# A decoder layer on one NeuronCore: the order of two products, a remade weight difference, a chunk-wise end and other banks for the query

## The chip, the cores and the metric

The kernel runs on one core of one Trainium2 chip, as one program without collectives. What is compared is the device time of one execution, in microseconds, as the median of several executions. One further execution was recorded by the profiler; the traces and rows below are of that one. About 0.2% of the time, 2.3 us, is what a measurement of this kernel can tell from no change.

## The reference, cut to what matters

One layer on a residual stream x of 1024 tokens by 1024 features, all in float32.

```
h = rmsnorm(x, pre_mix_g);  z = h @ w_in            # 7 slices of 512 columns
q, f, i, g, gate_b, gate_c, conv_h = split(z)
mix_a = hgrn2(q, f, i, g)                           # 4 heads of 128, gated recurrence
mix_b = gate_b * causal_dwconv(gate_c * conv_h, conv_w)
x = x + rmsnorm(concat(mix_a, mix_b) @ w_out, post_mix_g)
h = rmsnorm(x, pre_ffn_g)
u = causal_dwconv(h @ ffn_w_up, ffn_conv_w)         # 1024 -> 2 * 2816, three taps
gate, val = split(u)
y = (silu(gate) * val) @ ffn_w_down                 # 2816 -> 1024
x = x + rmsnorm(y, post_ffn_g)
```

## The kernel before

Every float32 operand is split into a high part `hi` (type float32r, written by ScalarE) and a low part `lo = x - hi` (written by VectorE; `split`, L112). A product is then three matmuls, hi·hi, hi·lo and lo·hi (`mm3_fm` L166, `mm3_tm` L171). In both, one of the three needs the low part of the weights, and that one comes after a matmul that needs only the high part. A matmul writes a tile of 128 by 512, which fills one PSUM bank.

**Start (L600 to L642).** The input is normalised late: the first projections work on x times its gain, and the factor r of each token comes in when a projection is read out. `gemm_quad` (L184) computes 512 columns in four banks. Its weights come in four pairs of 128 rows; a pair's high and low parts (`h_f`, `l_f` for the forget gate, `h_q`, `l_q` for the query) live in one of three slots, so the third query pair takes the slot that the last forget pair leaves. While the forget projection f runs, the sum of squares is made (`stats_by_feature`, L258, matmuls `pc`), `rstd` (L139) turns it into r by a chain of eleven small VectorE operations on `rt` and `rs`, and `by_token` (L272) lays r out along the tokens: VectorE makes four diagonal tiles `dg`, four 128x128 products `pb` sum them (eight pieces in the trace), and ScalarE copies the result to `rb`. `evac_f` (L296) multiplies the four banks of f by `rb` into `tf` and makes F and the keys by two sigmoids each. Then q follows in the same pool of four banks, `ps_mm`; the other four banks, `ps_ax`, serve small results (`aux`, L104). The second half of the tokens gets its row by `by_token_through_dram` (L283): a write of r to DRAM, element by element, and a read that broadcasts it to all partitions.

**Up projection (L680 to L910).** Both feed-forward matmuls use a scheme with seven products P1 to P7 on 2x2 blocks (the Strassen-Winograd scheme), with sums and differences of blocks as operands. A group n handles a 128-column slice of the gate and one of the values. Its tiles `g` (`pG`) and `v` (`pV`) are "two" tiles of two banks each (`two_banks`, L740). Every product is 12 matmuls. P1 and P2 of the groups 0 to 7 are done ahead, during the output projection, and parked (`ahead`, L704); in the loop `take_back` (L767) copies them into `g`. `mid` (L787) runs P6 into g[:,1], copies that out (`snap`, tile `s`), runs P5 into v[:,1], adds v[:,0] = v[:,1] + s (L799), runs P7 into g[:,1], copies again and adds v[:,1] += s (L802). In the next turn of the loop `tail_1` (L815) adds P4 to g[:,1] and reads out the gate (`conv`, silu), and `tail_2` (L822) adds P3 to v[:,0], reads out the value, multiplies both, and after every second group writes the seven left operands of the down projection to DRAM (`down_operands`, L832; L840 to L842 on SyncE's queue).

**Down projection (L913 to L1069).** The seven products run in the order 1, 2, 6, 7, 5, 3, 4 over eleven 128-row blocks, in six granules `GR` of two rows, one of them of one row (L913). `down_granule` (L973) loads the left operand `s`, and `right_operand` (L947) loads raw blocks b11, b12, b21, b22 of the weights (`raw_w`, five slots) and makes differences: T1 = b12 - b11 in product 1 (for the first two granules, whose product-1 operands were loaded early, in product 2), T2 = b22 - T1 and T3 = b22 - b12 in product 2. T1, T2 and T3 stay in memory; products 5, 6 and 7 use them. Results go into two "two" tiles: chunks 0 and 1 in `pXv` or `pYv`, chunks 2 and 3 in `pXg` or `pYg`. The last product, 4, takes its last three granules as one run (`joined=3`): first all their blocks for chunks 0 and 1, then for chunks 2 and 3. `result` (L1015) reads a chunk (ScalarE squares with a sum, `jy`; VectorE multiplies by the gain, `my`), and `finish_rows` (L1028) does `rstd`, adds the residual (two operations L1037 a chunk) and stores.

**What sets the order.** The framework plans it before the run: on each engine it takes, by its own estimate of times, the instruction that is ready and stands first in the program (`high_priority` goes ahead). On the chip each engine then follows that list strictly, with waits for what it reads or overwrites. Nearly all loads and stores are issued by SyncE (SP), in one list.

Of the kernel before, what the change touches and what calls it, by code (L numbers as in the profile page):

```python
# [17 lines left out]
P = 128  # L18
D = 1024
# [22 lines left out]
def decoder_kernel(ctx: ExitStack, tc: tile.TileContext, x, xT, w_sq, w_cv, w_out, w_up, w_dn,  # L42
# [27 lines left out]
    nc.vector.tensor_scalar(neg[:], vec[:, V_PREF : V_PREF + KH], -1.0, None, ALU.mult)  # L70
# [113 lines left out]
    def gemm_quad(src, act, name, token_major, groups, order=None, pieces=1, rate=1, hooks=None, queue=None,  # L184
                  gains=None):

        order = order or list(range(len(act)))
        pss = [ps_mm.tile([P, TH], F32, tag="mm", name=f"p_{name}_{j}") for j in range(4)]
        ws, i0 = {}, 0
        for gi, n in enumerate(groups):  # L190
            ks = range(i0, i0 + n)
            for i in ks:
                if i // 2 not in ws:
                    ws[i // 2] = load_w(src[order[i] // 2], (P, 2, TH), f"{name}_{i // 2}", pieces,
                                         queue if i == 0 else None, (gains or {}).get(order[i] // 2))
            for j in range(4):
                for i in ks:
                    whi, wlo = (w[:, i % 2, :] for w in ws[i // 2])
                    js = slice(j * P, (j + 1) * P)
                    ahi, alo = act[order[i]]  # L200
                    first, last = i == 0, i == len(act) - 1
                    if token_major:
                        mm3_tm(pss[j][:], ahi[:, js], alo[:, js], whi, wlo, first, last)
                    else:
                        mm3_fm(pss[j][:], whi[:, js], wlo[:, js], ahi, alo, first, last)
                if (i0 + n) % 2 == 0 and j % (4 // rate) == 4 // rate - 1:
                    tick()
            i0 += n
            if hooks and gi in hooks:
                hooks[gi]()  # L210
        return pss
# [6 lines left out]


    lbt = zp.tile([P, 4, H], F32, name="lbt")  # L220
    lbp = vec[:, V_LB : V_LB + H]
    e_, s_, lb, oml = (lbt[:, i, :] for i in range(4))
    nc.vector.tensor_tensor(e_, lbp, lbp, ALU.subtract)
    nc.scalar.activation(e_, e_, AF.Exp)
    nc.vector.reciprocal(s_, e_)
    nc.vector.tensor_tensor(s_, s_, e_, ALU.mult)
    nc.vector.tensor_tensor(lb, s_, s_, ALU.subtract)
    nc.vector.tensor_scalar(oml, lb, -1.0, 1.0, ALU.mult, ALU.add)
# [384 lines left out]

    first = {}
# [8 lines left out]
    def scale_a_rows():  # L623
        with tc.high_priority():
            first["rows"] = by_token(0, first["r"])

    pss = gemm_quad(w_sq[0], Lazy(), "f0", False, (1, 1, 1, 1, 1, 1, 1, 1), pieces=2, queue=nc.scalar,
                    hooks={6: scale_a, 7: scale_a_rows})
    r0 = first["r"]
    rb0 = first["rows"]  # L630
    rq0 = for_values(0, r0)
    F0, UW0 = evac_f(0, pss, rb0)
    pss = gemm_quad(w_sq[1], act_a, "q0", False, PAIRS)
    evac_q(0, pss, rb0, UW0)
# [62 lines left out]
    AHEAD = 8  # L697

# [64 lines left out]
    def head_2(n):  # L763
        b = box[n]
        product(b["g"][:, 0], b.pop("x"), 0, 2)
# [49 lines left out]
    def tail_1(n):  # L815
        b = box[n]
        product(b["g"][:, 1], b["y"], 0, 4)
# [4 lines left out]
    def tail_2(n):  # L822
        b = box[n]
        product(b["v"][:, 0], b.pop("y"), 1, 3)
# [68 lines left out]
    for n in range(NF + 1):  # L893
# [8 lines left out]
        if n:  # L902
            tail_1(n - 1)
        if n >= AHEAD and not last:
            head_2(n)
        if n:
            tail_2(n - 1)
# [27 lines left out]
    def raw_w(kh, nh, i, n, name):  # L935
        t = ft("wr", (P, 2, TH), name, 5)
        nc.sync.dma_start(t[:, :n], w_dn[kh, nh, :, i : i + n])
        return t
# [7 lines left out]

    def right_operand(op, gi, i, n):  # L947

        nm = f"{op}_{gi}"
        if op == 1:  # L950
            b = raw_w(0, 0, i, n, f"b11_{nm}")
            t_1(gi, n, b, raw_w(0, 1, i, n, f"b12_{nm}"))
            return b
        if op == 2:
            b = raw_w(1, 0, i, n, f"b21_{nm}")
            b12 = raw_w(0, 1, i, n, f"b12_{nm}")
            if gi < EARLY:
                t_1(gi, n, raw_w(0, 0, i, n, f"b11_{nm}"), b12)
            b22 = raw_w(1, 1, i, n, f"b22_{nm}")
            t2 = ts[2, gi] = t_slot(2, gi, n)  # L960
            t3 = ts[3, gi] = t_slot(3, gi, n)
            nc.vector.tensor_tensor(t2[:], b22[:, :n], ts[1, gi][:], ALU.subtract)
            nc.vector.tensor_tensor(t3[:], b22[:, :n], b12[:, :n], ALU.subtract)
# [7 lines left out]
        return ts[{5: 1, 6: 2, 7: 3}[op], gi]  # L971

    def down_granule(op, gi):  # L973
        i, n = GR[gi]
        s = ft("sr", (P, 2, TH), f"s{op}_{gi}", 4)
# [10 lines left out]
    def down_product(op, pss, first=False, joined=0, made=()):  # L986
# [3 lines left out]
        for gis in runs:  # L990
            ks = [(gi, k, t) for gi in gis
                  for k, t in enumerate(made[gi] if gi < len(made) else down_granule(op, gi))]
            for cs in ((0, 1), (2, 3)):
# [34 lines left out]
    def finish_rows(hf, cs):  # L1028
        c0, c1 = cs[0], cs[-1] + 1
        r = rstd(ssq[hf][:, c0:c1], D, f"y{hf}{c0}", ssq[hf][:, 4 + c0 : 4 + c1])  # L1030
# [104 lines left out]
```

## Time and profile before

| | |
|---|---|
| median of 3 executions | 1139.5 us (1139.35 to 1140.95) |
| profiled execution: own time, span | 1138.99 us, 1137.2 us |
| TensorE matmul busy (PE) | 1109.6 us, 5096 matmuls |
| VectorE busy (DVE) | 838.4 us |
| ScalarE busy (ACT) | 512.6 us |
| mean granted TensorE clock | 0.994 |
| DMA | 163.03 MB, mean 143 GB/s |

The profiled execution's time is 1.8 us more than its span, which begins with the first recorded instruction. Busy times of the engines overlap. A matmul's end is modelled: its own duration of 0.39 us is more than the 0.227 us between two starts, so a busy PE is judged by the distance between starts and not by the busy time.

### The profile page before, as it was taken

What the parts mean: (1) busy time and instruction counts of PE and PEld (TensorE: products, weight loads), DVE (VectorE), ACT (ScalarE), POOL (GpSimd) and SP (SyncE); (2) the same over time, 40 slices, a digit from 0 to 9 for tenths busy, and PEclk for the clock granted to TensorE, in tenths of its full rate; (3) what the DMA queues carried; (4) which work ended last, traced back from release to release, by engine and by line L of the source; (5) the groups of instructions that cost most, each with busy time, mean ns of one, the idle gap of its engine ahead of it and who ended that gap; (6) DMA issues with size and microseconds to landing.
All of it is one profiled execution on the core that took longest, in us unless ns stands there. A gap on an engine that the chain in (4) does not pass through costs nothing.

```text
span 1137.2 us, 13444 instructions
## 1 busy us (share of the span) xinstructions
PE 1109.6 (98%) x5096; PEld 912.8 (80%) x5096; DVE 838.4 (74%) x1181; ACT 512.6 (45%) x750; POOL 9.7 (1%) x16
## 2 busy tenths in 40 slices
PE   8999999999999999999999999999999999999996
PEld 6878888888878888887777888888888877888884
DVE  8578767636687777387998987878887777744786
ACT  6543335425432337366555444444444433544441
POOL 2000000000000000000000000000000000000000
PEclk9999999999999999999999999999999999999998
DMA  8522223335322238174444323222331479735653
GB/s 292 172 78 74 75 93 113 119 95 201 101 66 86 82 111 260 59 256 167 164 168 168 111 94 139 102 75 102 131 110 51 153 282 334 280 102 168 202 165 132
DMA packets 54432, 163.03 MB, mean 143 GB/s; under 512 B 5856, under 2 KB 6112, under 8 KB 51424
## 3 DMA queue, kind: packets, MB, share of 16 engines
q1 hardware_dynamic: 53936, 161.57, 41.5%
q8 instruction: 40, 0.66, 0.2%
q10 hardware_dynamic: 432, 0.61, 0.2%
q14 instruction: 24, 0.20, 0.1%
HBM read 127.82 MB, written 34.34 MB: 143 GB/s over the span
## 4 chain that ended last, share of the span: by engine, by line
PE 86%; DVE 6%; DMA 3%; ACT 3%; issue 2%; DVEq 0%; SPq 0%; ACTq 0%
PE pG L167 8%; PE pG L169 8%; PE pG L168 8%; PE pV L167 4%; PE pV L169 4%; PE pV L168 4%; PE sl L382 2%; PE p_wo L174 2%; PE p_wo L173 2%; PE p_wo L172 2%; DMA b<-w_dn 2%; PE pXv L173 2%; PE pXv L174 1%; PE pXv L172 1%; PE p_ch L169 1%
## 5 line engine op out<-in xcount | busy, mean ns | idle before, releaser
L113 ACT CAST hs<-s 128x1024 fp32r<-128x1024 f32 (+1 forms) x40 | 39.1, 976 | 91.9 <-PE pXg L173 35.9
L114 DVE TENSOR_TENSOR ls<-s,hs 128x1024 fp32r<-128x1024 f32 (+1 forms) x40 | 45.2, 1129 | 44.4 <-ACT hs L113 44.2
L114 DVE TENSOR_TENSOR l_b<-w,h_b 128x1024 fp32r<-128x1024 f32 x22 | 26.9, 1223 | 33.6 <-ACT h_b L113 33.6
L167 PE MATMUL pG<-uhi,h_x 128*128 128x512 f32 x112 | 44.4, 396 | 0.0
L168 PE MATMUL pG<-ulo,h_x 128*128 128x512 f32 x112 | 44.3, 395 | 0.0
L169 PE MATMUL pG<-uhi,l_x 128*128 128x512 f32 x112 | 44.1, 394 | 0.0
L749 ACT COPY s<-pG 128x512 f32<-128x512 f32 x44 | 25.7, 583 | 40.8 <-PE pG L169 40.6
L114 DVE TENSOR_TENSOR l_t<-t,h_t 128x1536 fp32r<-128x1536 f32 x22 | 38.6, 1755 | 5.9 <-ACT h_t L113 5.7
L811 ACT ACTIVATE g<-pG,vec 128x1024 f32<-128x1024 f32 x22 | 24.5, 1116 | 34.2 <-PE pG L169 34.2
L167 PE MATMUL pG<-c4h,h_b 128*128 128x512 f32 x88 | 35.4, 402 | 4.7 <-ACT s L749 4.7
L820 ACT ACTIVATE g<-g 128x1024 f32<-128x1024 f32 x22 | 23.3, 1061 | 36.3 <-DVE g L813 36.1
L113 ACT CAST h_t<-t 128x1536 fp32r<-128x1536 f32 x22 | 32.6, 1484 | 14.4 <-DVE t L783 9.6
L113 ACT CAST h_x<-w 128x1024 fp32r<-128x1024 f32 x14 | 14.7, 1052 | 47.4 <-DMA w<-w_up 47.4
L383 DVE COPY_PREDICATED S<-m_lev,sl 128x512 f32<-128x512 uint8 x28 | 24.9, 890 | 14.7 <-PE sl L382 14.7
L369 ACT COPY lhs<-UW 128x512 f32<-128x512 f32 x28 | 18.6, 663 | 37.2 <-DVE UW L390 37.2
L382 PEld LDWEIGHTS sl<-UW,lhs 128*128 128x128 f32 x224 | 28.8, 190 | 7.3 <-issue 4.1
L169 PE MATMUL pG<-c4h,l_b 128*128 128x512 f32 x88 | 34.6, 393 | 0.0
L167 PE MATMUL pV<-c3h,h_b 128*128 128x512 f32 x88 | 34.5, 392 | 0.0
L167 PE MATMUL pG<-c7h,h_t 128*128 128x512 f32 x88 | 34.4, 391 | 0.1
L169 PE MATMUL pV<-c3h,l_b 128*128 128x512 f32 x88 | 34.4, 391 | 0.0
L169 PE MATMUL pG<-c7h,l_t 128*128 128x512 f32 x88 | 34.3, 390 | 0.0
L168 PE MATMUL pG<-c4l,h_b 128*128 128x512 f32 x88 | 34.3, 390 | 0.0
(351 smaller groups left out, 3524.1 us busy)
## 6 DMA issues: line engine op xcount, KB each, us to landing
w<-w_up SPq DMA_DIRECT2D x22, 1024.0 KB, 4.8
s<-s_d SPq DMA_DIRECT2D x33, 512.0 KB, 3.9
b<-w_dn SPq DMA_DIRECT2D x33, 512.0 KB, 6.0
s_d<-g SPq DMA_DIRECT2D x22, 512.0 KB, 2.9
s_d<-S SPq DMA_DIRECT2D x11, 768.0 KB, 3.4
r_wo<-w_out SPq DMA_DIRECT2D x16, 512.0 KB, 3.5
xT<-xT SPq DMA_DIRECT2D x16, 256.0 KB, 4.0
r_q<-w_sq SPq DMA_DIRECT2D x8, 512.0 KB, 4.3
```

Source lines behind the costliest of these rows:

```text
L113: nc.scalar.copy(hi, src)
L114: nc.vector.tensor_tensor(lo, src, hi.bitcast(F32), ALU.subtract)
L167: nc.tensor.matmul(ps, whi, ahi, start=first, stop=False, skip_group_check=more)
L168: nc.tensor.matmul(ps, whi, alo, start=False, stop=False, skip_group_check=more)
L169: nc.tensor.matmul(ps, wlo, ahi, start=False, stop=last, skip_group_check=more)
L172: nc.tensor.matmul(ps, ahi, whi, start=first, stop=False, skip_group_check=more)
L173: nc.tensor.matmul(ps, ahi, wlo, start=False, stop=False, skip_group_check=more)
L174: nc.tensor.matmul(ps, alo, whi, start=False, stop=last, skip_group_check=more)
L382: nc.tensor.matmul(pv[:, :, i], lhs[:, i, :], rhs, start=True, stop=True)
L383: nc.vector.copy_predicated(view(S, 2 * X, o + h, (X - h, 2), (2 * h, n), (1, h)), m_lev[:, li].rearrange("p x g (b h) -> p x (g b) h", h= ...
L749: nc.scalar.copy(t[:], ps)
L811: nc.scalar.mul(a[:], c, wc[2])
```

## The change

Five things are edited.

1. In the groups that ran ahead (loop turns 1 to 7) P3 stands in front of P4 in the program; after them P4, gate, P2 of the next group, P3, value keep their order.
2. T3 is no longer kept. Product 7 loads b12 and b22 again and subtracts. T1 of the first two granules is made in product 1, with loads of their own, at granules 2 and 3, so that product 2 loads only b21 and b22. The slots of raw weights go from 5 to 8 and those of left operands from 4 to 6.
3. The joined last granules of product 4 run chunk by chunk, and the last half of the rows is finished one chunk at a time, each with its own `rstd`. The two sums of `rstd` change places.
4. The query projection goes into the banks of `ps_ax`, and the row r of the first half goes through DRAM, read out with `evac_f` after the first pair of the query.
5. The constants of the lower bound (`lbt`) and `neg` are made later in the program.

```
     def gemm_quad(..., gains=None, banks=None):
-        pss = [ps_mm.tile([P, TH], F32, tag="mm", name=f"p_{name}_{j}") for j in range(4)]
+        pss = [banks(f"p_{name}_{j}") if banks else ps_mm.tile([P, TH], F32, tag="mm", name=f"p_{name}_{j}")
+               for j in range(4)]
...
     def scale_a_rows():
-        with tc.high_priority():
-            first["rows"] = by_token(0, first["r"])
+        first["rows"] = by_token_through_dram(0, first["r"])
+        first["FU"] = evac_f(0, pss, first["rows"])
     pss = gemm_quad(w_sq[0], Lazy(), "f0", False, (1, 1, 1, 1, 1, 1, 1, 1), pieces=2, queue=nc.scalar,
-                    hooks={6: scale_a, 7: scale_a_rows})
+                    hooks={6: scale_a})
     r0 = first["r"]
-    rb0 = first["rows"]
+    qss = gemm_quad(w_sq[1], act_a, "q0", False, PAIRS, hooks={0: scale_a_rows}, banks=aux)
+    rb0, (F0, UW0) = first["rows"], first["FU"]
     rq0 = for_values(0, r0)
-    F0, UW0 = evac_f(0, pss, rb0)
-    pss = gemm_quad(w_sq[1], act_a, "q0", False, PAIRS)
-    evac_q(0, pss, rb0, UW0)
+    evac_q(0, qss, rb0, UW0)
...
-        if n:
-            tail_1(n - 1)
-        if n >= AHEAD and not last:
-            head_2(n)
-        if n:
-            tail_2(n - 1)
+        if n and n < AHEAD:
+            product_3(n - 1)
+            product_4(n - 1)
+            gate(n - 1)
+            value(n - 1)
+        elif n:
+            product_4(n - 1)
+            gate(n - 1)
+            if not last:
+                head_2(n)
+            product_3(n - 1)
+            value(n - 1)
...
-        t = ft("wr", (P, 2, TH), name, 5)
+        t = ft("wr", (P, 2, TH), name, 8)
...
+    def early_t1(gi):
+        i, n = GR[gi]
+        t_1(gi, n, raw_w(0, 0, i, n, f"b11_t{gi}"), raw_w(0, 1, i, n, f"b12_t{gi}"))
     def right_operand(op, gi, i, n):
         if op == 1:
+            if gi < 2 * EARLY:
+                early_t1(gi - EARLY)
             b = raw_w(0, 0, i, n, f"b11_{nm}")
             t_1(gi, n, b, raw_w(0, 1, i, n, f"b12_{nm}"))
             return b
         if op == 2:
             b = raw_w(1, 0, i, n, f"b21_{nm}")
-            b12 = raw_w(0, 1, i, n, f"b12_{nm}")
-            if gi < EARLY:
-                t_1(gi, n, raw_w(0, 0, i, n, f"b11_{nm}"), b12)
             b22 = raw_w(1, 1, i, n, f"b22_{nm}")
             t2 = ts[2, gi] = t_slot(2, gi, n)
-            t3 = ts[3, gi] = t_slot(3, gi, n)
             nc.vector.tensor_tensor(t2[:], b22[:, :n], ts[1, gi][:], ALU.subtract)
-            nc.vector.tensor_tensor(t3[:], b22[:, :n], b12[:, :n], ALU.subtract)
+            return b
+        if op == 7:
+            b12 = raw_w(0, 1, i, n, f"b12_{nm}")
+            b = raw_w(1, 1, i, n, f"b22_{nm}")
+            nc.vector.tensor_tensor(b[:, :n], b[:, :n], b12[:, :n], ALU.subtract)
             return b
...
-        s = ft("sr", (P, 2, TH), f"s{op}_{gi}", 4)
+        s = ft("sr", (P, 2, TH), f"s{op}_{gi}", 6)
...
-            for cs in ((0, 1), (2, 3)):
+            for cs in ((0,), (1,), (2,), (3,)) if len(gis) > 1 else ((0, 1), (2, 3)):
...
-        r = rstd(ssq[hf][:, c0:c1], D, f"y{hf}{c0}", ssq[hf][:, 4 + c0 : 4 + c1])
+        r = rstd(ssq[hf][:, 4 + c0 : 4 + c1], D, f"y{hf}{c0}", ssq[hf][:, c0:c1])
...
-    for cs in ((0, 1), (2, 3)):
-        for c in cs:
-            result(1, 0, c, bx[c])
-        finish_rows(1, cs)
+    for c in range(NC_H):
+        result(1, 0, c, bx[c])
+        finish_rows(1, [c])
```

`product_4` and `product_3` are the matmuls that `tail_1` and `tail_2` began with, `gate` and `value` the rest of them.

More of the change, by code (lines that the diff above doesn't have):

```diff
@@ L69, in decoder_kernel @@
     neg = cp.tile([P, KH], F32, name="neg")
-    nc.vector.tensor_scalar(neg[:], vec[:, V_PREF : V_PREF + KH], -1.0, None, ALU.mult)
     nc.scalar.activation(warm[:], ones[:, 0:1], AF.Exp)
@@ L184, in gemm_quad @@
     def gemm_quad(src, act, name, token_major, groups, order=None, pieces=1, rate=1, hooks=None, queue=None,
-                  gains=None):
+                  gains=None, banks=None):
         order = order or list(range(len(act)))
-        pss = [ps_mm.tile([P, TH], F32, tag="mm", name=f"p_{name}_{j}") for j in range(4)]
+        pss = [banks(f"p_{name}_{j}") if banks else ps_mm.tile([P, TH], F32, tag="mm", name=f"p_{name}_{j}")
+               for j in range(4)]
         ws, i0 = {}, 0
@@ L217, in zt @@
         return pool.tile(list(shape), dt, tag=tag, bufs=bufs, name=name or tag)
[L220 to L228, printed above, removed]
     S = zt("S", (P, 2, 8, C))
@@ L612, in __getitem__ @@
             return act_a[k]
+    lbt = zp.tile([P, 4, H], F32, name="lbt")
+    lbp = vec[:, V_LB : V_LB + H]
+    e_, s_, lb, oml = (lbt[:, i, :] for i in range(4))
+    nc.vector.tensor_tensor(e_, lbp, lbp, ALU.subtract)
+    nc.scalar.activation(e_, e_, AF.Exp)
+    nc.vector.reciprocal(s_, e_)
+    nc.vector.tensor_tensor(s_, s_, e_, ALU.mult)
+    nc.vector.tensor_tensor(lb, s_, s_, ALU.subtract)
+    nc.vector.tensor_scalar(oml, lb, -1.0, 1.0, ALU.mult, ALU.add)
     first = {}
@@ L697, in decoder_kernel @@
     AHEAD = 8
+    nc.vector.tensor_scalar(neg[:], vec[:, V_PREF : V_PREF + KH], -1.0, None, ALU.mult)
     ah_w = zh.tile([P, 2, 2, KH, P], F32, tag="F", name="ah_w")
@@ L813, in conv, with product_4, product_3, gate @@
         nc.vector.scalar_tensor_tensor(a[:, 2:], c[:, : T - 2], wc[0], a[:, 2:], ALU.mult, ALU.add)
-    def tail_1(n):
+    def product_4(n):
+        product(box[n]["g"][:, 1], box[n]["y"], 0, 4)
+    def product_3(n):
+        product(box[n]["v"][:, 0], box[n]["y"], 1, 3)
+    def gate(n):
         b = box[n]
-        product(b["g"][:, 1], b["y"], 0, 4)
         g = b["o"] = ft("ag", (P, T), f"g{n}", 3, pool=pa[0])
@@ L820, in tail_1, with value @@
         nc.scalar.activation(g[:], g[:], AF.Silu)
-    def tail_2(n):
+    def value(n):
         b = box[n]
-        product(b["v"][:, 0], b.pop("y"), 1, 3)
         v = ft("av", (P, T), f"v{n}", 2, pool=pa[0])
@@ L970, in right_operand @@
             return b
-        return ts[{5: 1, 6: 2, 7: 3}[op], gi]
+        return ts[{5: 1, 6: 2}[op], gi]
     def down_granule(op, gi):
         i, n = GR[gi]
-        s = ft("sr", (P, 2, TH), f"s{op}_{gi}", 4)
+        s = ft("sr", (P, 2, TH), f"s{op}_{gi}", 6)
         nc.sync.dma_start(s[:, :n], s_d[:, S_AT[op], i : i + n])
```

## The prediction

> **What bounds the kernel now.** I read the page first, then who waited for whom on PE, then timelines of the places that the diff touches.
>
> ```profile
> span 1137.2 us, 13444 instructions
> ...
> PE 1109.6 (98%) x5096; PEld 912.8 (80%) x5096; DVE 838.4 (74%) x1181; ACT 512.6 (45%) x750; POOL 9.7 (1%) x16
> ```
> ```profile
> PE pG L167 <- ACT s L749: 4.7, 7, 0.7
> ...
> PE pb L278 <- DVE dg L277: 1.9, 1, 1.9
> ```
>
> PE bounds it, and the number of large matmuls stays. So the change can only win what PE loses between matmuls and in the tail behind the last one, about 1% of the span. Of PE's waits, the seven on `s` and the one at `pb` are what edits 1 and 4 aim at. I take each stage's loss from distances between starts.
>
> **Start (edits 4 and 5).**
>
> ```profile
> 23.57 0.48 PE L169 MATMUL p_f<-hi,l_f 128*128 128x512 f32 x1
> ...
> 26.61 0.39 PE L167 MATMUL p_f<-hi,h_f 128*128 128x512 f32 x1
> 28.87 1.16 PE L278 MATMUL pb<-dg,ones 128*128 128x128 f32 x8 [1.87 <-DVE dg L277]
> 29.78 0.48 PE L168 MATMUL p_f<-lo,h_f 128*128 128x512 f32 x1
> ...
> 34.45 0.39 PE L167 MATMUL p_q<-hi,h_q 128*128 128x512 f32 x1
> ```
> ```profile
> 4.48 0.17 DVE L70 TENSOR_SCALAR neg<-vec 128x4 f32<-128x4 f32 x1 [1.86 <-DMA vec<-vecs]
> ...
> 5.69 0.75 DVE L244 SCALAR_TENSOR_TENSOR lo<-xT,vec,hi 128x512 fp32r<-128x512 f32 x1
> ...
> 28.04 0.16 DVE L155 SCALAR_TENSOR_TENSOR rs_x<-rt_x,rs_x 128x4 f32<-128x4 f32 x1
> ...
> 32.68 2.66 DVE L303 TENSOR_TENSOR tf<-p_f,rb 128x512 f32<-128x512 f32 x4 [2.15 <-PE p_f L169]
> ...
> 38.67 1.22 DVE L114 TENSOR_TENSOR l_q<-r_q,h_q 128x1024 fp32r<-128x1024 f32 x1
> ```
>
> `pb` stands amid the forget matmuls. From 26.61 to 29.78 are 3.17 us where 0.23 is normal (the pitch is worked out below): 2.9 us go with `pb`. q then starts at 31.5. The constants leave the way of the first low part, 4.48 to 5.69; they can slip back in while it waits for ScalarE, so between 0 and 0.4 us, and I take 0. The other banks cost nothing: the next user of those banks is work that needs q read out anyway.
>
> The change adds a wait. `tf` on VectorE now waits for a row that travels through DRAM; behind it stand the scalings of F and the keys and perhaps `l_q`. On SP, the read waits for the write; behind it are loads for the projections after q, needed when q ends at 53 (31.5 + 4 x 5.46 us, below). The rows for both trips come from the second half of the tokens, then one for a full queue:
>
> ```profile
> rd<-rs_x SPq DMA_DIRECT2D x1, 2.0 KB, 8.7
> ```
> ```profile
> DMA to landing us min/median/max: 3.9/3.9/3.9
> ```
> ```profile
> xs<-x SPq DMA_DIRECT2D x1, 512.0 KB, 7.5
> ```
>
> The row lands at R = 28.2 + 8.7 + 3.9 = 40.8, up to 3.6 later if one of the trips meets a queue like that of `xs` (7.5 - 3.9), so 44.4; I take the middle, 42.4. From `tf` to the end of the next `l_q` were 38.67 + 1.22 - 32.68 = 7.2 us. A query pair takes 24 matmuls, 5.46 us; the third needs its low part at 31.5 + 10.9 + 0.45 = 42.9, the fourth at 48.3. The third's slot is free at 31.5, so it can be split before the row is there; the fourth's only at 37, so it will stand behind. Stall: R - 41.1, 0 to 3.3, and I take 1.3. Start: 2.9 - 1.3 = 1.6 us gained, between -0.4 and 3.3.
>
> The Trainium skill (DMA: Bandwidth & Descriptors, section "Anatomy of one DMA") gives a fixed cost of about 2 us for any DMA; by it the row would land near 33, the stall would be nil and the sum 1.3 better. The 8.7 us for 2 KB differ, and the measurement decides; the same page (Rules for kernel authors) says that a strided last dimension becomes one descriptor per element, as in this write.
>
> **P3 before P4 (edit 1).** One group, with P7's last matmul first:
>
> ```profile
> 561.09 0.39 PE L169 MATMUL pG<-c7h,l_t 128*128 128x512 f32 x1
> 562.15 0.50 PE L167 MATMUL pG<-c4h,h_b 128*128 128x512 f32 x1 [0.68 <-ACT s L749]
> 562.49 0.39 PE L168 MATMUL pG<-c4l,h_b 128*128 128x512 f32 x1
> ...
> 565.00 0.39 PE L167 MATMUL pV<-c3h,h_b 128*128 128x512 f32 x1
> ...
> 567.73 0.39 PE L167 MATMUL pG<-c2h,h_t 128*128 128x512 f32 x1
> ```
> ```profile
> 562.13 0.70 DVE L802 TENSOR_TENSOR pV<-pV,s 128x512 f32<-128x512 f32 x1
> ```
>
> P3 takes 2.73 us for 12 matmuls, a pitch of 0.2275. The gap costs (562.49 - 561.09) - 2 x 0.2275 = 0.945, seven times 6.6 us. P3 could fill it if it were free to start. Its bank v[:,0] is, but L802, ahead of it in the program, writes v[:,1] of the same tile, and waits for the same `s`. Does that hold P3? The tail has rows for two banks of one tile, chunk 2 and chunk 3:
>
> ```profile
> 1125.23 0.39 PE L174 MATMUL pXg<-hw,ls 128*128 128x512 f32 x1
> ...
> 1125.91 0.39 PE L174 MATMUL pXg<-hw,ls 128*128 128x512 f32 x1
> ```
> ```profile
> 1126.40 0.60 ACT L1021 ACTIVATE jy<-pXg 128x512 f32<-128x512 f32 x1 [4.67 <-PE pXg L174]
> ...
> 1127.19 0.68 DVE L1022 TENSOR_TENSOR my<-pXg,pg 128x512 f32<-128x512 f32 x1
> ...
> 1127.91 0.60 ACT L1021 ACTIVATE jy<-pXg 128x512 f32<-128x512 f32 x1 [0.83 <-DVE my L1022]
> ```
>
> Chunk 2's last matmul ends at 1125.62, chunk 3's at 1126.30. The reader of chunk 2, on an idle engine, starts only after the latter; chunk 3's reader waits for VectorE's reading of chunk 2. So waits go by the whole tile, and P3 waits for L802. Nor does the planner hold ready work back:
>
> ```profile
> 940.85 0.39 PE L172 MATMUL pYv<-hw,hs 128*128 128x512 f32 x1
> 941.08 0.39 PE L172 MATMUL pYg<-hw,hs 128*128 128x512 f32 x1
> 941.66 0.50 PE L173 MATMUL pYv<-lw,hs 128*128 128x512 f32 x1 [0.20 <-DVE lw L114]
> ```
>
> While `lw` is missing it puts in a matmul of chunk 2, though chunk 0's next stands first. Had P3 been free at 561.3, it would stand in the gap already. I expect P4 to start at `s` as before, some matmuls of it, then P3, then the rest: gain 0. Ends: 0.3 better, or 7 x 0.33 = 2.3 worse if P3 comes one matmul too early for L802 (0.22 wait and the 0.11 by which a first matmul's pitch, 0.34, is longer).
>
> **Down projection (edit 2).**
>
> ```profile
> 920.00:960.00 40.00, 37.16 (x150) 28.34 (x149) 28.66 (x28) 14.01 (x17) 0.00 (x0) 0.96 0.96 350
> ...
> 985.00:1050.00 65.00, 65.00 (x289) 53.81 (x288) 30.06 (x30) 29.15 (x36) 0.00 (x0) 1.00 0.47 149
> ```
> ```profile
> 975.80 0.39 PE L172 MATMUL pXv<-hw,hs 128*128 128x512 f32 x1
> ```
> ```profile
> 915.63 0.38 SPq L840 DMA_DIRECT2D s_d<-g  x1
> 916.11 1.29 SPq L937 DMA_DIRECT2D b<-w_dn  x2
> ```
> ```profile
> b<-w_dn SPq DMA_DIRECT2D x33, 512.0 KB, 6.0
> ```
>
> P2 runs from 940.85 to 975.80, 34.95 us for 132 matmuls that need 30.0: 4.9 lost, and the clock was granted 0.96. DMA is full there: 0.96 busy at 350 GB/s. A granule of P2 has 5.46 us and loads four blocks of 0.524 MB, 6.0 us at that rate, and five (7.5 us) in the first two; with two blocks fewer there, and one fewer elsewhere, it is 4.5 us. So DMA stops being P2's limit. What stays is the wait at 941.08 to 941.66, 0.4. In P1 the loads grow by 2.1 MB, 6 us of DMA, which may fit in before the store L840 at 915.63, where the raw loads now go on, and VectorE gets two more subtractions, 1.2 us each; I put one on PE's path. P7 takes 5.8 MB more in 30 us, to about 290 GB/s, and six subtractions, 6 us; by the row of 985 to 1050 VectorE is under half busy, so both hide; without that cover P7 would lose like P2 did. Net: 4.9 - 0.4 - 1.2 = 3.3 us, ends 0 and 5.
>
> **Tail (edit 3).**
>
> ```profile
> 1129.24 0.16 DVE L147 TENSOR_SCALAR rt_y<-ssy 128x2 f32<-128x2 f32 x1
> ...
> 1131.40 2.74 DVE L1037 SCALAR_TENSOR_TENSOR my<-my,rs_y,xr 128x512 f32<-128x512 f32 x4
> ```
>
> From the last matmul's end to the span's end are 10.9 us. As whole tiles wait, chunk 2 is read no earlier than before. But its `rstd` (2.16 us) can start at 1127.8, after its own `my`, not at 1129.24; chunk 3's `my` slips in (0.6) and chunk 3's chain runs in the waits of the other: the four L1037 start at 1130.4, 1.0 earlier. If the two chains run one after the other, VectorE has two more us of small steps, once for chunks 0 and 1 and once for 2 and 3: 0.9 to 1.9 later. As the planner fills waits, I take 1.0 gained.
>
> **Sum.** 1.6 + 0 + 3.3 + 1.0 = 5.9 off the profiled 1138.99: 1133.1. The median before stands 0.5 above that execution, so 1133.6; with its terms' ends this case reaches from 1129 to 1137.5.
>
> **The rivals.** (a) Banks are kept apart after all and P3 starts at P7's end: up to 6.6 more, but about 3 if VectorE, which these groups load to nine tenths, falls behind: 1127 to 1130.6.
>
> ```profile
> 500.00:640.00 140.00, 135.22 (x591) 108.90 (x590) 127.37 (x141) 80.48 (x97) 0.00 (x0) 1.00 0.46 163
> ```
>  The Trainium skill (PSUM — Partial Sum Buffer, section "PSUM bank collisions raise a hardware error") finds accesses to different banks clean, so the chip would allow it. The rows of the tail speak against it in this program.
> (b) The other side: in VectorE's list the third query pair stands behind `tf`. For it: `l_q` at 38.67 came after the forget gate's work before too. Against: by the planner's order, 14 matmuls between 23.57 and 28.87 cover `rstd` and `dg`, 3.2 us, so two trips of more than 5 us end after the slot is free. Then PE stalls R + 7.2 - 42.9: 5.1 at R = 40.8 and 8.7 at 44.4, plus 1.6 of clock (the 4% of 40 us of P2's row), less the 1.3 already counted: 1139.0 to 1142.6. From R = 43.6 on it is slower than 1141.8; two full queues, R = 48, give 1146.
> (c) T1's loads stand ahead of granule 2's in SP's list, which then come after L840: 916.1 + 6.0 + 2.4 for the splits (1.22 the low part, the high part about as much) is 924.5. They are needed near 921 (940.85 less 84 matmuls, 19.1 us, and P1's waits): 3.5 lost, P2's gain gone: 1137.
>
> **How the numbers follow.** The forecast has 0.50, (a) 0.10, (b) 0.27, (c) 0.13. The bound of 2.3 us (0.2%) puts the forecast (but 0.03) and (a) in faster, (c) half and half, (b) 0.16 in same and 0.11 in slower: faster 0.64, same 0.25, slower 0.11. The range 1127.5 to 1141 leaves out some of (a) and the upper half of (b).
>
> **What would show it.** No `pb`, and forget matmuls 0.23 apart up to q. P4's first matmul still waiting for `s`, with P3 among its matmuls; if P3 starts within 0.3 us of P7's last, (a) holds. The second `l_q` wait on PE near 43 (b) or 48 us. P2 within 31 us, DMA busy clearly below 0.96 there. L1037 of chunk 3 ending under 8 us after the last matmul. The forecast is wrong if PE waits over 3 us in the query or in P1.

## The result and the profile after

| | before | after |
|---|---|---|
| median | 1139.4 us (4 runs, 1138.8 to 1141.0) | 1150.9 us (4 runs, 1150.6 to 1151.2) |
| profiled execution's span | 1137.2 us | 1148.7 us |
| mean granted clock | 0.994 | 0.989 |

The ratio is 1.0098, with a 95% interval of 1.0081 to 1.0116: the change costs 11.5 us, where 5.9 us of gain were forecast. (In the runs below, one of the nine executions of d2_down_t1_in_p2 took 3968.6 us; no trace shows why, and its ratio is taken without it.) The page and the waits of PE after the change (microseconds in all, how often, the longest):

```profile
span 1148.7 us, 13452 instructions
...
PE 1112.8 (97%) x5088; PEld 914.8 (80%) x5088; DVE 837.7 (73%) x1199; ACT 511.4 (45%) x749; POOL 10.5 (1%) x16
```
```profile
PE sd L343 <- ACT kqh L112: 6.4, 1, 6.4
PE pG L166 <- ACT s L749: 4.7, 7, 0.7
...
PE pXv L171 <- ACT hw L112: 2.6, 1, 2.6
...
PE p_q L166 <- ACT h_q L112: 1.7, 1, 1.7
PE p_q L168 <- DVE l_q L113: 1.1, 2, 0.6
```

The wait at `pb` is gone, the seven waits for `s` stand unchanged, and there are new waits in the query (the two rows of `p_q`) and in the first scores (`sd`); the one for `hw` in P1 was 0.2 before. To see what each is worth, set the starts of PE's stages side by side; the last column is what the stage itself lost (+) or gained.

| from, to | before | after | difference |
|---|---|---|---|
| span's start, query's first matmul | 34.45 | 31.44 | -3.0 |
| query | 21.76 | 26.93 | +5.2 |
| i projection up to `sd` | 5.45 | 11.99 | +6.5 |
| `sd` to the first `sl` | 12.82 | 15.68 | +2.9 |
| `sl` to P2's first matmul | 866.37 | 870.79 | +4.4 |
| P2 | 34.95 | 30.45 | -4.5 |
| P6 to the last matmul's start | 150.11 | 149.63 | -0.5 |
| last matmul's start to the span's end | 11.29 | 11.79 | +0.5 |

The differences add up to the 11.5 of the spans. The first 90 us lose 11.6; the later gains and losses cancel. A stage of one execution has its own scatter: in five runs below that have the start of the kernel before unchanged (d1, d2, p2, t1, t2), the query begins between 33.98 and 35.52. Windows of that part (busy time of PE, PEld, DVE, ACT, POOL; then granted clock, DMA share and GB/s):

```profile
31.44:58.37 26.93, 24.11 (x97) 18.86 (x96) 13.17 (x29) 14.48 (x21) 1.17 (x1) 0.94 0.79 149
58.37:76.00 17.63, 11.25 (x38) 8.46 (x37) 7.98 (x10) 5.34 (x8) 0.00 (x0) 0.81 0.51 109
```

The second stretch also shows why a stall costs more than its own length: the granted clock is 0.81 (0.51 from 70.3 to 76.0, behind the stall at `sd`), and matmuls that follow the stall are 0.43 us apart where 0.23 is normal.

**The first stall: SP, ACT and DVE around it.** SP's issues (start, time to issue), in the kernel before and in the changed one, then the changed one's ScalarE and VectorE lists, with the idle time ahead of an instruction and who ended it:

```profile
24.14 0.97 SPq L268 DMA_DIRECT2D xs<-x  x2
```
```profile
27.91 0.39 SPq L274 DMA_DIRECT2D rd<-rs_x  x1
28.35 1.15 SPq L257 DMA_DIRECT2D xs<-x  x2
39.23 0.33 SPq L276 DMA_DIRECT2D rb<-rd  x1
...
52.05 0.38 SPq L274 DMA_DIRECT2D rd<-rs_x  x1
53.22 1.46 SPq L130 DMA_DIRECT2D r_i<-w_sq  x2
```
```profile
42.03 1.06 ACT L258 ACTIVATE xs<-xs 128x1024 f32<-128x1024 f32 x1 [12.92 <-DMA xs<-x]
...
43.09 1.03 ACT L112 CAST h_q<-r_q 128x1024 fp32r<-128x1024 f32 x1
...
66.75 1.04 ACT L112 CAST h_i<-r_i 128x1024 fp32r<-128x1024 f32 x1 [8.18 <-DMA r_i<-w_sq]
```
```profile
44.15 1.23 DVE L113 TENSOR_TENSOR l_q<-r_q,h_q 128x1024 fp32r<-128x1024 f32 x1 [14.68 <-ACT h_q L112]
45.29 2.48 DVE L292 TENSOR_TENSOR tf<-p_f,rb 128x512 f32<-128x512 f32 x4
...
51.97 1.23 DVE L113 TENSOR_TENSOR l_q<-r_q,h_q 128x1024 fp32r<-128x1024 f32 x1
```

The write of r (512 elements of 4 bytes) goes out at 27.91; the read back follows only at 39.23, 11.3 us later. Two of the four loads `xs`, for the sums of squares of the second half, are issued behind the write; in the kernel before they went out at 24.14. ScalarE waits 12.92 us for the third of them, and its list has the third query pair behind that square. So `h_q` comes at 43.09, `l_q` at 44.15, and PE stands. `tf`, which waits for the row, comes after this `l_q`: it is not what held it. The fourth pair is another matter: its `l_q` (51.97, done at 53.20) stands behind `tf` and the forget gate's work, and PE needed it at 48.3, had the query run on from 31.44 without a stall. The third pair's stall and the slow matmuls behind it hide most of that wait. Of the query's 5.2 us, about 2.7 are the wait at the third pair, 1.6 matmuls 0.43 us apart behind it, 0.9 what is left of the wait at the fourth.

What moved on DMA meanwhile (40 slices of 0.9 us from 24 us on), and the times from issue to landing of what was issued between 26 and 41 us:

```profile
GB/s 328 246 360 159 64 11 100 36 0 32 32 36 27 27 23 18 36 36 369 325 209 193 355 385 360 230 344 239 314 382 264 5 2 59 77 0 0 64 27 18
```
```profile
xs<-x SPq DMA_DIRECT2D x2, 512.0 KB, 14.0
...
rd<-rs_x SPq DMA_DIRECT2D x1, 2.0 KB, 11.3
```

From 27.6 to 40.2 us (the 5th to the 18th figure) it is 100 at most and mostly 18 to 36, though two loads of half a megabyte are waiting; then it is back at 369.

**The second stall.** As the second half's squares are late, its own row is written at 52.05 and not at 44.1, now just ahead of two `r_i` pairs (the lines above). For what was issued from 51 to 57 us:

```profile
r_i<-w_sq SPq DMA_DIRECT2D x2, 512.0 KB, 14.2
...
rd<-rs_x SPq DMA_DIRECT2D x1, 2.0 KB, 13.1
```

ScalarE waits 8.18 us for the pair (66.75 above), and behind it in its list stands `kqh`, for which PE waits 6.4 us at `sd`.

**P1, P2 and P3/P4.** SP and ScalarE at the end of P1, then PE there:

```profile
916.44 0.43 SPq L947 DMA_DIRECT2D b<-w_dn  x1
927.10 0.38 SPq L844 DMA_DIRECT2D s_d<-g  x1
...
932.91 1.55 SPq L947 DMA_DIRECT2D b_t<-w_dn  x2
```
```profile
940.29 0.62 ACT L112 CAST hw<-b 128x512 fp32r<-128x512 f32 x1 [2.62 <-DMA b<-w_dn]
```
```profile
587.07 0.39 PE L168 MATMUL pG<-c7h,l_t 128*128 128x512 f32 x1
588.14 0.50 PE L166 MATMUL pG<-c4h,h_b 128*128 128x512 f32 x1 [0.68 <-ACT s L749]
...
589.63 0.40 PE L166 MATMUL pV<-c3h,h_b 128*128 128x512 f32 x1
...
940.96 0.50 PE L171 MATMUL pXv<-hw,hs 128*128 128x512 f32 x1 [2.61 <-ACT hw L112]
...
956.83 0.39 PE L171 MATMUL pYv<-hw,hs 128*128 128x512 f32 x1
```

SP stands from 916.87 to 927.10 in front of the store L844 (L840 in the kernel before); the second pair of loads for T1 (`b_t`, 932.91) and those of the later granules come after it, and PE waits. P2, from 956.83 to 987.28, has no stall but one of 0.4 us at its start. DMA, however, is no less busy there than before: 0.93 of the time at 347 GB/s, where P2 of the kernel before had 0.93 and 340. At 588.14 P4 still comes first and waits for `s`; P3 follows after six of its matmuls.

**The tail.**

```profile
1131.25 0.39 PE L173 MATMUL pXv<-hw,ls 128*128 128x512 f32 x1
```
```profile
1131.73 0.60 ACT L1037 ACTIVATE jy<-pXv 128x512 f32<-128x512 f32 x1 [6.42 <-PE pXv L173]
```
```profile
1137.76 1.41 DVE L1053 SCALAR_TENSOR_TENSOR my<-my,rs_y,xr 128x512 f32<-128x512 f32 x2
1139.10 0.68 DVE L1038 TENSOR_TENSOR my<-pXg,pg 128x512 f32<-128x512 f32 x1
```

Chunk 0's square waits for the last product in its tile, which is chunk 1's. And when chunk 2 is there (last matmul 1136.91), VectorE is still at chunk 1's row end until 1139.1.

### The profile page after: what moved, and what is told of

The parts are those of the page before. It is cut to its first block, busy times and chain, and to the rows that moved or that the text cites. A ratio compares the mean times of both kernels' runs of the same rounds, so it can differ in the third digit from the quotient of the medians.

```text
span 1148.7 us, 13452 instructions
## 1 busy us (share of the span) xinstructions
PE 1112.8 (97%) x5088; PEld 914.8 (80%) x5088; DVE 837.7 (73%) x1199; ACT 511.4 (45%) x749; POOL 10.5 (1%) x16
## 4 chain that ended last, share of the span: by engine, by line
PE 87%; DVE 4%; DMA 4%; ACT 2%; issue 1%; SPq 0%; DVEq 0%; ACTq 0%
PE pG L166 8%; PE pG L168 8%; PE pG L167 7%; PE pV L166 4%; PE pV L168 3%; PE pV L167 3%; PE sl L371 2%; PE p_wo L173 2%; PE p_wo L172 2%; PE p_wo L171 2%; PE pXv L172 2%; PE pXv L171 2%; PE pXv L173 2%; PE pYv L172 1%; PE pXg L171 1%
## 5 line engine op out<-in xcount | busy, mean ns | idle before, releaser
L166 PE MATMUL pG<-uhi,h_x 128*128 128x512 f32 x112 | 44.4, 396 | 0.0
L168 PE MATMUL pG<-uhi,l_x 128*128 128x512 f32 x112 | 44.1, 394 | 0.0
L749 ACT COPY s<-pG 128x512 f32<-128x512 f32 x44 | 25.7, 585 | 29.7 <-PE pG L168 29.6
L168 PE MATMUL pV<-c1h,l_t 128*128 128x512 f32 x88 | 34.3, 389 | 0.0
L167 PE MATMUL pV<-c1l,h_t 128*128 128x512 f32 x88 | 34.2, 389 | 0.0
```

Source lines behind the costliest of these rows:

```text
L166: nc.tensor.matmul(ps, whi, ahi, start=first, stop=False, skip_group_check=more)
L167: nc.tensor.matmul(ps, whi, alo, start=False, stop=False, skip_group_check=more)
L168: nc.tensor.matmul(ps, wlo, ahi, start=False, stop=last, skip_group_check=more)
L749: nc.scalar.copy(t[:], ps)
```

## Experiments

Theory after the traces: the write of r element by element is the cause of both early stalls, by what it holds up; the other edits together are worth nothing. The rivals were the trip through DRAM as such (`tf` in front of the query's split), the other banks, and the loads in P1. Each row was measured beside the kernel before on the same chip; ratios are to it.

| run | median, us | ratio, 95% interval |
|---|---|---|
| s1_start_undone | 1140.0 | 0.9994 (0.9983 to 1.0005) |
| s2_pool_queue | 1140.3 | 0.9998 (0.9986 to 1.0009) |
| s3_whole_rows | 1137.8 | 0.9977 (0.9968 to 0.9986) |
| s4_banks | 1140.2 | 1.0000 (0.9991 to 1.0010) |
| s5_second_half | 1141.2 | 1.0008 (0.9997 to 1.0019) |
| d1_down | 1139.2 | 0.9996 (0.9985 to 1.0007) |
| d2_down_t1_in_p2 | 1137.1 | 0.9975 (0.9962 to 0.9988) |
| p2_split_banks | 1137.0 | 0.9964 (0.9951 to 0.9978) |
| t1_tail | 1142.2 | 1.0017 (1.0004 to 1.0030) |
| t2_tail_pairs | 1141.9 | 1.0013 (1.0000 to 1.0026) |
| b1_best | 1128.8 | 0.9897 (0.9880 to 0.9914) |
| b2_tail_one_bank | 1127.2 | 0.9885 (0.9865 to 0.9905) |

The kernel before had medians of 1140.97 (s1 to s4), 1139.97 (d1, d2, p2, t1), 1140.29 (s5, t2, b1) and 1140.81 us (b2).

**s1_start_undone.** The start of the kernel before in the changed kernel.

```
-    qss = gemm_quad(w_sq[1], act_a, "q0", False, PAIRS, hooks={0: scale_a_rows}, banks=aux)
+    F0, UW0 = evac_f(0, pss, rb0)          # rb0 from by_token, as before
+    pss = gemm_quad(w_sq[1], act_a, "q0", False, PAIRS)
```

> The changed kernel with its start put back (row of 1/rms through PE, query in f's banks), all else as changed. Theory, from the two traces: up to the first use of sl the changed kernel is 11.56 us late and nothing after that gives or takes more than 5, which cancels; without the new start the time falls by 11.5, to 1139.4 (1138.4 to 1140.4), and the last four edits together are worth 0. Rival: the late start also shifts later stages against their loads, so that undoing it leaves a part of the loss: over 1141.

As the theory has it: edit 4 is the whole loss, and what is left of the change is worth nothing that can be measured (0.9994).

**s2_pool_queue.** Only the issuing queue of the two small transfers is other.

```
-        nc.sync.dma_start(rd.rearrange("c p -> p c"), r[:])
+        nc.gpsimd.dma_start(rd.rearrange("c p -> p c"), r[:])
...
-        nc.sync.dma_start(rb[:], rd.rearrange(...))
+        nc.gpsimd.dma_start(rb[:], rd.rearrange(...))
```

> The changed kernel with the row's write and its read back issued by POOL in place of SP, in both halves. Theory (the 2 KB write in 512 elements of 4 bytes holds SP's queue, so that xs, and behind it on ACT the third query pair, come late; then rd1 holds the r_i loads): the write still takes 8 to 11 us, but xs lands before 36, the third query pair's stall of 5.2 and the stall of 6.4 at sd go with the half clock behind them (2.6), 1137 to 1141. Rival (the trip through DRAM as such, tf in front of the query's split on DVE): the row comes as late as before, the stall at the third pair stays, 1145 to 1151.

The time is the theory's. The stall at the third pair is gone and the one at `sd` shrinks to 0.9 us; another 0.9 us stand at the fourth pair. But the trace does not bear out the theory's wording. POOL's and VectorE's lists, and landings of what was issued from 26 to 41 us:

```profile
29.27 0.92 POOL L274 DMA_DIRECT2D rd<-rs_x  x1 [0.91 <-DVE rs_x L154]
...
40.20 0.60 POOL L276 DMA_DIRECT2D rb<-rd  x1 [9.59 <-DMA rd<-rs_x]
```
```profile
46.81 2.48 DVE L292 TENSOR_TENSOR tf<-p_f,rb 128x512 f32<-128x512 f32 x4 [10.04 <-DMA rb<-rd]
```
```profile
r_i<-w_sq SPq DMA_DIRECT2D x2, 512.0 KB, 11.9
xT<-xT SPq DMA_DIRECT2D x4, 256.0 KB, 12.6
```

The write takes as long as ever, and the loads that SP issued meanwhile took 12 us too, although it stood in another queue. So it is not SP's queue alone that is held: loads in flight beside the write are. What the other queue brought is order. SP's list no longer waits for r, so the last two `xs` were issued at 24.7 and not at 28.35, ahead of the write; and the second row's write went out at 40.8, long before the last two `r_i` pairs (50.45). The rival keeps a part: the fourth pair's `l_q` stands behind `tf`, which waits for the row, and that is the 0.9 us there. The Trainium skill (DMA: Bandwidth & Descriptors, section "Issuing engines are not separate DMA queues") says that transfers of all issuing engines run on the same 16 DMA engines and interleave. The 12.6 us agree with the first half; of an even interleaving this case shows little.

**s3_whole_rows.** One small matmul turns r into four rows, and the write is four lines of 512 bytes.

```
+        pt = aux(f"pt{hf}", (NC_H, C))
+        nc.tensor.matmul(pt[:], r[:], ident[:], start=True, stop=True)
+        nc.vector.tensor_copy(rr[:], pt[:])
...
-        nc.sync.dma_start(rd.rearrange("c p -> p c"), r[:])
+        nc.sync.dma_start(rd[:], rr[:])
```

> The changed kernel with r turned by one PE matmul into 4 rows of 128, so that the write is 4 lines of 512 bytes and not 512 elements; still on SP, in both halves. Theory (it is the element-wise form that costs): the write lands in under 4 us and not 8 to 11, what stands behind it on SP is not held, 1137 to 1141. Rival (any write and read back on SP in that place holds the loads behind it, since SP waits for the landing before the read): a landing of 8 us or more and 1146 to 1151.

```profile
32.04 0.33 SPq L282 DMA_DIRECT2D rd<-rr  x1
...
34.24 0.33 SPq L130 DMA_DIRECT2D r_i<-w_sq  x1
34.66 0.38 SPq L284 DMA_DIRECT2D rb<-rd  x1
```

The read follows 2.6 us behind the write, on SP, with loads between them; those issued from 31 to 42 us land in 5.1 (`xT`) and 5.9 us (`r_i`). No stall is left in the query or at `sd`, and the query ends 2.7 us earlier than in the kernel before. Same trip through DRAM, same queue: the form of the write was the cost of the trip and of the loads behind it. The order has changed as well, since the turned row comes later: the last two `xs` (24.37) stand ahead of the first write, and the second row's write goes out only at 198.3. No run has the four lines in the old places. s2, with the old form and the order changed, is already back at 1140.3, so most of the 11.5 us goes with the order alone. The Trainium skill (DMA: Bandwidth & Descriptors, section "Rules for kernel authors") says that a strided last dimension is lowered to one descriptor per element and should be made contiguous. The traces agree: from the write's issue to the read's are 11.3 us in the changed kernel and 2.6 here.

**s4_banks.** The query in the other banks, the row by PE as before.

```
-    pss = gemm_quad(w_sq[1], act_a, "q0", False, PAIRS)
+    qss = gemm_quad(w_sq[1], act_a, "q0", False, PAIRS, hooks={0: scale_f}, banks=aux)
```

> The changed kernel with the query in the other four banks, but the row made on PE as in the kernel before: the banks alone. Theory: the 2.9 us in front of the query are PE waiting for pb's input, not for banks; they stay, no DRAM trip, 1138.5 to 1140.5. Rival (the banks held the query back in the kernel before): 1135 to 1138.

The query starts at 35.23, about as before, and runs its 21.76 us without a stall: the banks alone are worth nothing, and the rival falls.

**s5_second_half.** As s3, but for the second row only.

```
+        if hf == 0:
+            nc.sync.dma_start(rd.rearrange("c p -> p c"), r[:])
+        else:
+            nc.sync.dma_start(rd[:], rows_of(1, r)[:])
```

> The changed kernel with the second half's row alone written as four whole lines (its turn on PE then stands late, so no write of 512 elements is left ahead of the r_i loads); the first half's row is as changed. Theory (two separate stalls: the first row's write holds xs, the second row's write holds the r_i pairs): the third query pair's stall of 5.2 stays, the stall of 6.4 at sd and its half clock go, sd starts 2 to 3 us later than in the kernel before and not 8.7, 1141.5 to 1144. Rival (r_i is late because SP and its queue were held by the first write alone): the stall at sd stays, 1148 to 1151.

```profile
r_i<-w_sq SPq DMA_DIRECT2D x2, 512.0 KB, 4.3
```
```profile
63.83 0.39 PE L353 MATMUL sd<-kqh,ones_r 128*128 128x512 f32 x1
```

The second row's write now goes out at 203.1, behind all of this; so the run shows what the write does to these loads by standing ahead of them, and not what its form does. The same two loads, issued at the same time (53.2), land in 4.3 us and not in 14.2; the wait at `sd` is gone, and `sd` starts 2.2 us later than in the kernel before, which is the query's loss net of its earlier start. The two stalls are separate, and the second one was the larger: without it `sl` starts at 76.65 and not at 86.04.

**d1_down and d2_down_t1_in_p2.** The down edit alone, then the same with T1 left in P2:

```
         if op == 1:
-            if gi < 2 * EARLY:
-                early_t1(gi - EARLY)
...
         if op == 2:
             b = raw_w(1, 0, i, n, f"b21_{nm}")
+            if gi < EARLY:
+                early_t1(gi)
```

> The kernel before with the down edit alone (T3 made in P7, T1 of the first two granules in P1 with loads of their own, eight and six slots). Theory from the two traces: P2 loses its stalls (minus 4.5), P1 gains as much because the loads for T1 stand ahead of granule 3's on SP's queue (plus 4.5), P6 gives 0.7: 1138.5 to 1139.8 and P1 34 to 35 us long, P2 30.5. Rival: P1's loss in the changed kernel came from the late start and not from the loads: P1 30.3, and 1134 to 1136.

> As the run before it, but T1 of the first two granules stays in P2, as in the kernel before; T3 alone has moved. Theory (it is P1's four added loads that cost): P1 is 30.3 us again, P2 keeps one subtraction more and some of its stall, 31 to 33 us, 1135 to 1138. Rival (P2's stall in the kernel before was the four loads a granule of its first two granules, not T3): P2 stays at 34 to 35 us and the time at 1139.

First matmuls of P2 and of P6, in d1, then in d2:

```profile
945.54 0.39 PE L172 MATMUL pYv<-hw,hs 128*128 128x512 f32 x1
...
976.00 0.39 PE L172 MATMUL pXv<-hw,hs 128*128 128x512 f32 x1
```
```profile
941.89 0.39 PE L172 MATMUL pYv<-hw,hs 128*128 128x512 f32 x1
...
973.00 0.39 PE L172 MATMUL pXv<-hw,hs 128*128 128x512 f32 x1
```

P2 is 30.46 us in d1, 31.11 in d2, 34.95 in the kernel before. From the first `pXv` of P1 to P2 are 41.50 us in d1, 36.89 in d2 and 36.94 before. So d1's gain in P2 is given back in P1, and it is the four added loads that cost; with T1 left in P2 nearly all of the gain is kept. Whether it comes from T3's move is not shown, for d2 has the added slots too. By its trace DMA moves 401 GB/s in P2 (340 before), and between 920 and 980 SP's weight loads waited 22.4 us for VectorE to free something in the kernel before, 1.8 us from 920 to 975 in d2. A run with the slots alone would tell.

**p2_split_banks.** The kernel before with edit 1, and P3's pair as two tiles.

```
+    def two_tiles(name):
+        return [ps_v.tile([P, TH], F32, tag="one", name=f"{name}{i}")[:] for i in range(2)]
...
-        v = b["v"] = two_banks(ps_v, f"pV{n}")
+        v = b["v"] = two_tiles(f"pV{n}")
```

> The kernel before with P3 ahead of P4 in the groups that ran ahead, and P3's two banks made two tiles of one bank each, so that P3's bank need not wait for what is written to the other; the value convolution then runs by halves (four VectorE and two ScalarE instructions where there were two and one). Theory (the gain of this edit is lost to the wait on the whole two-bank tile): P3's twelve matmuls stand ahead of all of P4's, PE's wait for the snapshot (4.7 in all over seven groups) goes, minus 3 to minus 4.7, 1134 to 1136.5. Rival (VectorE at 91% in this stage becomes the bound with the added instructions, or P3's bank is late itself): the waits move to another row, 1138.5 to 1141.

```profile
562.94 0.39 PE L169 MATMUL pG<-c7h,l_t 128*128 128x512 f32 x1
563.17 0.39 PE L167 MATMUL pV<-c3h,h_b 128*128 128x512 f32 x1
```

P3 follows P7 after 0.23 us, and the stage from the first `pV` to P2 is 414.1 us where it was 418.6. Of these 4.5 us, 3.1 come in the turns of the seven groups, where the gaps came to 6.6. VectorE is busy 87.5 of 95 us there, and PE waits for it twice in a product that follows (`l_t`, 1.2 in all). The other 1.4 come from P1, which runs its 132 matmuls in 30.0 us; P1's tile of two banks was split as well, and no run separates that. So the order of P3 and P4 was lost to the shape of the tile. Whether the split alone, with P4 first in the program, would gain as much was not run.

**t1_tail and t2_tail_pairs.** The tail edit alone; then its chunk order (and the exchanged sums of `rstd`), with the row ends in pairs as before. This line is in both:

```
-            for cs in ((0, 1), (2, 3)):
+            for cs in ((0,), (1,), (2,), (3,)) if len(gis) > 1 else ((0, 1), (2, 3)):
```

> The kernel before with the tail alone (last three granules chunk by chunk, each chunk's row ends for itself). Theory from the two traces: the span's end comes 11.4 us after the last matmul and not 10.9, plus 0.5 (0 to 1), 1139.5 to 1140.5. Rival (the prediction: rstd chains interleave under the last products): 9.9 us after the last matmul, 1138 to 1138.8.

> The kernel before with the last three granules chunk by chunk, but row ends in pairs of chunks as before: half of the tail edit. Theory (what costs in the tail is four separate rstd chains and row ends on VectorE, which stand in front of the last chunks' products): the end comes 10.9 us or less after the last matmul, 1138.5 to 1139.8. Rival (it is the chunk by chunk order that costs): 11.4 or more, 1140 to 1142.

Both ratios lie within the 0.2% that can't be told from no change; what follows rests on one trace each. From the last matmul's start to the span's end are 11.88 us in t1 and 11.98 in t2, 11.29 before. So my theory for t2 falls: by the traces it is the order that costs, not the four chains. When the first pair is read, in t2 and in the kernel before:

```profile
1123.64 0.60 ACT L1021 ACTIVATE jy<-pXv 128x512 f32<-128x512 f32 x1 [7.12 <-PE pXv L174]
```
```profile
1119.60 0.60 ACT L1021 ACTIVATE jy<-pXv 128x512 f32<-128x512 f32 x1 [5.08 <-PE pXv L174]
```

That is 5.2 us ahead of the last matmul (1128.82) in t2, 6.3 before (1125.91). In chunk order the planner fills the time until the last granules' operands are there with five matmuls of chunk 2: behind the pair's last one, at 1123.15, stand 25 matmuls (5.67 us) of chunks 2 and 3, which have 30. And chunk 0, done some fifteen matmuls before chunk 1, isn't read before chunk 1 is done. The tail explains 0.6 of t1's 1.9 us; where the rest of that median comes from the profiled execution doesn't show.

**b1_best and b2_tail_one_bank.** What gained, together; then the tail with the two-bank tile first and the two one-bank tiles singly at the end.

```
-            for cs in ((0, 1), (2, 3)):
+            for cs in ((2, 3), (0,), (1,)) if len(gis) > 1 else ((0, 1), (2, 3)):
```

> The parts that gained, put together: the changed start with whole lines, P3 ahead of P4 with P3's two banks as two tiles, T3 made in P7 with T1 left in P2, the tail of the kernel before. Theory (the gains lie in different stages and add up): minus 2.6, minus 4.1 and minus 2.9 against the kernel before, 1130 (1128.5 to 1132). Rival (a gain in one stage is given back in a later one): over 1133.

> As the run before it, with the tail edit in another form: the last three granules run chunks 2 and 3 together first (they share a two-bank tile), then chunk 0, then chunk 1 (each a tile of its own), and the row ends follow that order. Theory (the tail edit failed because ScalarE's square of a chunk waits for the last product of its whole two-bank tile, so an early chunk was of no use): chunk 0's square starts as its own products end, 3.4 before chunk 1's, and the span ends 9.8 to 10.6 after the last matmul starts where the kernel before has 11.3, 1128 against 1128.75. Rival (VectorE's own work, four row ends and the rstd chains, sets the end whatever the order): 11.3 or more, 1129 to 1130.

b1 is 11.5 us faster than the kernel before; by its trace what stands ahead of the first `pV` gives 1.9, from there to P2 4.3, P2 4.2, what follows 0.9. For b2, chunk 0's last product and the two squares:

```profile
1111.06 0.39 PE L173 MATMUL pXv<-hw,ls 128*128 128x512 f32 x1
```
```profile
1111.55 0.60 ACT L1060 ACTIVATE jy<-pXv 128x512 f32<-128x512 f32 x1 [1.26 <-PE pXv L173]
...
1114.95 0.60 ACT L1060 ACTIVATE jy<-pXv 128x512 f32<-128x512 f32 x1 [2.71 <-PE pXv L173]
```

Now chunk 0 is read as its own products end, 3.4 us ahead of chunk 1, and the end comes 10.2 us after the last matmul's start instead of 11.1 in b1. The two medians' intervals overlap; the 0.9 us are read from the traces. b2 beats both kernels: 1127.2 us.

## Why the prediction was wrong, point by point

By stages, the start was forecast to gain 1.6 and lost 11.6, the down projection to gain 3.3 and gained 0.6 (with P1, P2 and what follows up to the last matmul), the tail to gain 1.0 and lost 0.5. The ends of the terms, added up, reach from 1129.9 to 1144.1, and not from 1129 to 1137.5 as the sum has it; the measured 1150.9 lies outside both.

**Start.** The 2.9 us for `pb` came (3.0). The step that failed is the stall: "The third's slot is free at 31.5, so it can be split before the row is there", and, of SP, "behind it are loads for the projections after q, needed when q ends at 53". The slot was free; but behind the write on SP stood `xs` as well, which is not for those projections, and whose squares stand ahead of the third query pair on ScalarE. The step named VectorE's list and SP's, and not ScalarE's. The whole stall was put at the fourth pair, at 1.3 us; measured were 5.2, begun at the third.

The larger loss was not in the sum at all: the second row's write moved from 44.1 to 52.05, ahead of the `r_i` pairs, and cost 6.5 us, and 2.9 behind them, where the clock was low. The prediction had the row of that write (8.7 us for 2 KB) and used it as the time until r is back, not as a time in which other loads hardly move.

The landing R was mis-sized too. It was estimated at 40.8 to 44.4 and taken as 42.4; the write took 11.3 instead of 8.7 and the read 5.5 instead of 3.9, so the row was there at 44.7, and `tf` started at 45.29, right behind the third pair's `l_q`. By the prediction's own R - 41.1 that is a stall of 3.6 at the fourth pair, even without one at the third; its `l_q` was done 4.9 us after 48.3. So the wait for the row was there as told, but taken too small, and no run separates it from the third pair's in this order. Rival (b) gave the place (third query pair) and a stall of 5.1 to 8.7, with another cause: `tf` came behind that `l_q`. That its 1.6 us of clock match the slow matmuls in the query is luck, for they were taken from another stage. That a DRAM trip alone isn't to blame, s3 shows. The 2 us that the prediction gives from the Trainium skill (DMA: Bandwidth & Descriptors, section "Anatomy of one DMA") are told there of DMAs that GpSimd (POOL) issues; issued from its queue, in s2, the write took 10.8.

**P3 before P4.** Right, with its reason: gain 0, P4 first at `s`, then P3; p2 shows that the wait on the whole tile is what holds it, and that rival (a), in a kernel that splits the tile, is worth 3.1 us in the seven groups by the trace, near the "about 3" that it had for a busy VectorE.

**Down projection.** P2's term came out (4.9 to vanish but for 0.4; measured 4.5), but not its sign: DMA was to be clearly below 0.96 in P2, and its share there is 0.93 in both kernels. Whether fewer loads or more slots brought the gain stays open. P1's was mis-sized: 1.2 us for one subtraction, where four loads in SP's list cost 4.5 (d1). "Which may fit in before the store L840" failed: half of the loads came behind that store. Rival (c) was this mechanism, placed at granule 2 and priced 3.5; the wait fell on the granule of one row.

**Tail.** Forecast 1.0 gained, measured 0.5 lost. It was right that chunk 2 is read no earlier. The chains of chunks 2 and 3 did interleave: from chunk 2's `my` to the span's end are 9.6 us where they were 10.0. What failed is that `my`'s start: the first pair is read 1.1 us later against the last matmul in the new order, VectorE is at chunk 1's row end when chunk 2 arrives, and `my` begins 2.2 us after the last matmul's start and not 1.3.

**Constants.** Nothing seen of the 0 to 0.4 us: the first forget matmul starts at 7.03 against 6.92.

## What to carry to other kernels

Before moving a transfer, list for every queue and every engine what stands behind it, and for each of those what stands behind that; a stall here went from a DMA to a square on ScalarE to a weight split to PE. A small write element by element was priced here by what else was in flight during its time, not by its bytes; make it contiguous first. Where the framework waits by tile, give operands that are needed at different times tiles of their own, or an edit of the order finds nothing to move. And read a stage for all that holds it: here a second wait, for the row, lay hidden behind the first.

## What the runs showed of the hardware

The write of 512 single elements took 8.7 us in the kernel before, 11.3 and 13.1 in the changed one, 12.0 in s5, and 10.8 (median of two) from POOL's queue in s2; as four lines the read back could go out 2.6 us later. While it ran, loads of a quarter and half a megabyte took 12 to 14 us and not 4 to 7, whichever queue had issued it, and the core's DMA moved about 30 GB/s in the changed kernel. Its packets of 4 bytes all start between 28.5 and 29.6 in that trace; of the 95 larger packets that start from 28 to 40 us, 20 took over 3 us and one 9.3, while in s3 none from 27 to 50 us took over 2.0. How the write holds them stays open. A stall of 6.4 us on PE was followed by 2.9 us more of loss, at a granted clock of 0.81 in the window around it and 0.51 just behind it.
